# A dilated 3x3 convolution on one core: which transfers are whole, and how the last ten rows of the last image are stored

## The chip, the cores and the metric

The kernel runs on one core of one Trainium2 chip. The metric is the device time of one execution in microseconds (us); lower is better. Six runs of the kernel before stand beside a profile of one of its executions.

## The reference

Sixteen images of 64 channels and 64 x 64 pixels are convolved with 128 filters of 3 x 3 taps, dilation 2, zero padding 2, all in float32:

```python
batch, c_in, h, w, c_out, k, dilation = 16, 64, 64, 64, 128, 3, 2
x_pad = np.pad(x, ((0, 0), (0, 0), (pad, pad), (pad, pad)), mode='constant')   # pad = 2
output[b, co] += weight[co, ci, kh, kw] * x_pad[b, ci, kh*2:kh*2+h, kw*2:kw*2+w]
```

The input is 16.8 MB (1 MB an image), the output 33.6 MB (2 MB an image), the weights 0.3 MB. Every byte crosses between memory and the core once.

## The kernel before

**Pairs.** Two images of 64 channels fill the 128 partitions, so there are eight pairs, numbered 0 to 7 in the code. A pair's input is one tile `x32` of 128 partitions by 64 rows of 64 floats (2 MB). Its output is one tile `o_tiles[pb]` with the 128 output channels on the partitions and the two images side by side (4 MB).

**Groups.** A pair is worked off in four groups `g` of 16 image rows; the loop `for G in range(ngroups)` runs over 32 groups. In each, TensorE (PE) fills three PSUM tiles: `psP` (products that even and odd row blocks share), `psA` and `psB` (line 174). ScalarE (ACT) copies `psP` to `p_sb` (line 226). VectorE (DVE) adds `p_sb` to `psA` and `psB` and writes the output tile `osb` (line 233). ACT also casts the input from float32 to float16 (line 73), and DVE adds row blocks for the shared product (line 85). The order on each engine is written out by hand.

**Loads.** `load(pb, cuts, queue)` issues one transfer per piece between two cuts (line 64). The weights and pairs 0 (in two pieces), 1 and 2 are issued at the start by SyncE (SP). Pairs 3 to 7 are issued by ACT inside `casts`, as soon as the last cast of the pair three earlier has freed its `x32` tile. Pair 3 is loaded whole, pairs 4 to 7 in two halves of 32 rows.

**Stores.** `store(pb, m, r0, r1)` issues one transfer for rows `r0` to `r1` of image `m` of the pair, always over all 128 partitions, on the SP queue (line 187). Pairs 1 to 6 store two whole images after their last group. Pairs 0 and 7 store in halves: 32 rows of both images after the second group, and 32 rows of both after the fourth. In this kernel that makes 14 loads and 20 stores, 34 transfers.

**Who waits for whom.** SP issues the stores in program order, each after the DVE addition that completes its rows. There are three output tiles, so the first addition of a pair waits until the stores of the pair three earlier have landed. At the end SP waits for all stores to land (line 279 in the profile).

Of the kernel before, what the change touches and what calls it, by code (L numbers as in the profile page):

```python
# [10 lines left out]
def kernel(  # L11
# [7 lines left out]
    nc = tc.nc  # L19

    B, CI, H, W = x.shape
# [7 lines left out]
    P = 128  # L29
# [5 lines left out]
    HW = H * W  # L35
    GR = 16
    NG = H // GR
    NBLK = GR // 4
    NH = GR // 2 * W
    npairs = B // 2  # L40
    ngroups = npairs * NG
    chunk_rows = [(g * GR + (d if g else 0), min((g + 1) * GR + d, H)) for g in range(NG)]
    XF = 3
# [11 lines left out]
    out_img = out.rearrange("b o h w -> b o (h w)")  # L55
# [3 lines left out]
    x32_tiles, x16_tiles, xs_tiles, o_tiles = {}, {}, {}, {}  # L59

    def load(pb, cuts=(0, H), queue=nc.sync):
        x32_tiles[pb] = fpool.tile([P, HW], f32, tag="x32", name="x32")
        for lo, hi in zip(cuts[:-1], cuts[1:]):
            queue.dma_start(  # L64
                out=x32_tiles[pb][:, lo * W : hi * W], in_=x_pair[pb, :, lo * W : hi * W]
            )

    def cast(c):
        pb, g = divmod(c, NG)
        lo, hi = chunk_rows[g]  # L70
        if g == 0:
            x16_tiles[pb] = xpool.tile([P, HW], f16, tag="x16", name="x16")
        nc.scalar.copy(  # L73
            out=x16_tiles[pb][:, lo * W : hi * W], in_=x32_tiles[pb][:, lo * W : hi * W]
        )

    def rowsum(c):
        pb, g = divmod(c, NG)
        if g == 0:
            xs_tiles[pb] = sxpool.tile([P, HW // 2], f16, tag="xs", name="xs")  # L80
        v = x16_tiles[pb][:, g * GR * W : (g + 1) * GR * W].rearrange(
            "p (b e q) -> p b e q", e=2, q=2 * W
        )
        s = xs_tiles[pb][:, g * NH : (g + 1) * NH].rearrange("p (b q) -> p b q", q=2 * W)
        nc.vector.tensor_tensor(out=s, in0=v[:, :, 0], in1=v[:, :, 1], op=add)  # L85
# [33 lines left out]
    def turn(k):  # L119
# [24 lines left out]
        out=x16_tiles[0][:, 8 * W : 18 * W], in_=x32_tiles[0][:, 8 * W : 18 * W]  # L144
# [8 lines left out]
    def casts(G):  # L153
        for n in range(2 if G else 3):
            c = ahead[0]
            if c >= ngroups or c > G + (7 if c < 2 * NG else 3):
                return
            cast(c)
            ahead[0] += 1
            if c % NG == NG - 1 and c // NG + XF < npairs:  # L160
                k = c // NG + XF
                load(k, (0, H) if k == XF else (0, H // 2, H), queue=nc.scalar)

    def product(ps, src, kind, blk0, nblk, first, last):
        for j in (1, 0, 2):
            dw = (j - 1) * d
            o0, o1 = max(0, -dw), W - max(0, dw)
            t = kind * KW + j
            for hb in range(2):
                pp = slice(hb * CI, (hb + 1) * CI)  # L170
                rhs = src(pp, dw + o0, dw + o1)
                po = ps[:, hb * NH + blk0 * 2 * W : hb * NH + (blk0 + nblk) * 2 * W]
                po = po.rearrange("p (r w) -> p r w", w=W)[:, :, o0:o1]
                nc.tensor.matmul(  # L174
                    out=po,
                    lhsT=w_sb[pp, t * CO : (t + 1) * CO],
                    rhs=rhs,
                    start=first and j == 1,
                    stop=last and j == 2,
                )  # L180

    def blocks(x16, b0, n, e):
        v = x16.rearrange("p (b e r w) -> p b e r w", e=2, r=2, w=W)
        return lambda pp, c0, c1: v[pp, b0 : b0 + n, e, :, c0:c1]

    def store(pb, m, r0=0, r1=H):
        nc.sync.dma_start(
            out=out_img[2 * pb + m, :, r0 * W : r1 * W],
            in_=o_tiles[pb][:, m * HW + r0 * W : m * HW + r1 * W],
        )  # L190

    for G in range(ngroups):
        pb, g = divmod(G, NG)
        x16 = x16_tiles[pb]
        xs = xs_tiles[pb].rearrange("p (r w) -> p r w", w=W)
        if g == 0:
            o_tiles[pb] = opool.tile([P, 2 * HW], f32, tag="osb", name="osb")
        o = o_tiles[pb].rearrange("p (m b e q) -> p m b e q", m=2, e=2, q=2 * W)
        b0 = g * NBLK

        def summed():
            ps = ppool.tile([P, 2 * NH], f32, tag="p", name="psP")
            sv = lambda pp, c0, c1: xs[pp, g * GR // 2 : (g + 1) * GR // 2, c0:c1]
            product(ps, sv, 0, 0, NBLK, True, True)
            return ps

        if G:
            psP = summed()

        psA = apool.tile([P, 2 * NH], f32, tag="ab", name="psA")  # L210
        product(psA, blocks(x16, b0, NBLK, 1), 1, 0, NBLK, True, False)
        z = 1 if g == 0 else 0
        product(psA, blocks(x16, b0 + z - 1, NBLK - z, 1), 2, z, NBLK - z, False, True)

        psB = apool.tile([P, 2 * NH], f32, tag="ab", name="psB")
        product(psB, blocks(x16, b0, NBLK, 0), 3, 0, NBLK, True, False)
        z = 1 if g == NG - 1 else 0
        product(psB, blocks(x16, b0 + 1, NBLK - z, 0), 4, 0, NBLK - z, False, True)

        if not G:  # L220
            psP = summed()

        if not G:
            casts(0)
        p_sb = spool.tile([P, 2 * NH], f32, tag="psb", name="p_sb")
        nc.scalar.copy(out=p_sb, in_=psP)  # L226
        if G:
            casts(G)
        if G + 1 < ngroups:
            rowsum(G + 1)  # L230
        pv = p_sb.rearrange("p (m b q) -> p m b q", m=2, q=2 * W)
        for e, ps in ((0, psA), (1, psB)):
            nc.vector.tensor_tensor(  # L233
                out=o[:, :, b0 : b0 + NBLK, e],
                in0=ps.rearrange("p (m b q) -> p m b q", m=2, q=2 * W),
                in1=pv,
                op=add,
            )

        if pb in (0, npairs - 1):  # L240
            if g % 2 == 1:
                store(pb, 0, (g - 1) * GR, (g + 1) * GR)
                store(pb, 1, (g - 1) * GR, (g + 1) * GR)
        elif g == NG - 1:
            store(pb, 0)
            store(pb, 1)
# [37 lines left out]
```

## Time and profile before

| | |
|---|---|
| median of 6 runs | 127.77 us (127.59 to 127.89) |
| the profiled execution | 127.89 us, span 126.0 us, so 1.89 us lie outside the span |
| PE, DVE, ACT busy | 105.1, 90.4, 65.0 us |
| bytes moved | 50.78 MB, mean 403 GB/s over the span, in 4906 packets |
| SP's transfers | 3600 packets, 40.14 MB |
| ACT's transfers (pairs 3 to 7) | 1296 packets, 10.49 MB |
| stores | 12 of 2048 KB, 18.7 us from issue to landing; 8 of 1024 KB, 15.1 us |

The span runs from the first to the last instruction of the profiled execution. A transfer over 128 partitions moves one packet per partition: 16 KB for a whole image or pair, 8 KB for a half. The profile's rows of 40 slices show at a glance when the 16 DMA engines of the core were busy and what they moved. Each transfer also ends with a 4-byte packet on every engine that took part, which counts its completion.

### The profile page before, as it was taken

The numbers are of one execution on the slowest core, as the hardware profiler recorded it, in microseconds if no ns is written. First come the engines' busy times: TensorE is split into PE (matmuls) and PEld (weight loads), VectorE is DVE, ScalarE is ACT, GpSimd is POOL, SyncE is SP. The second block draws the span as 40 slices with busy tenths as digits, with TensorE's granted clock in tenths as the row PEclk, the third lists the DMA queues.
The fourth block names the chain that finished last, engine by engine and source line by source line (L and its number), as shares of the span: only waits on it lengthen the run. The fifth ranks groups of instructions, "written<-read, shape, count | busy, mean of one in ns | idle before, by whom it ended". The sixth has DMA issues, their size and how long they took to land.

```text
span 126.0 us, 2341 instructions
## 1 busy us (share of the span) xinstructions
PE 105.1 (83%) x1000; PEld 56.3 (45%) x1000; DVE 90.4 (72%) x103; ACT 65.0 (52%) x68; POOL 2.2 (2%) x8
## 2 busy tenths in 40 slices
PE   6994999999999999999999999999999999400000
PEld 2251555555555555555555555555555555100000
DVE  0560997988898888988969898887988987700000
ACT  4287894366656665666576666666666633000000
POOL 2400000000000000000000000000000000000000
PEclk9999999999999999999999999999999999965555
DMA  4999999999999999999999999999999999999970
GB/s 132 383 462 442 416 411 385 335 424 421 416 437 439 432 426 432 424 424 429 406 447 419 421 432 426 432 432 429 416 442 421 437 426 421 421 416 429 429 317 26
DMA packets 4906, 50.78 MB, mean 403 GB/s; under 512 B 544, under 2 KB 544, under 8 KB 800
## 3 DMA queue, kind: packets, MB, share of 16 engines
q1 hardware_dynamic: 3600, 40.14, 75.6%
q10 hardware_dynamic: 1296, 10.49, 20.4%
q8 instruction: 8, 0.13, 0.4%
q14 instruction: 2, 0.02, 0.0%
HBM read 17.07 MB, written 33.55 MB: 402 GB/s over the span
## 4 chain that ended last, share of the span: by engine, by line
PE 75%; DMA 6%; ACT 2%; issue 1%; DVE 1%; DVEq 1%; SPq 1%; ACTq 0%
PE psA L174 30%; PE psB L174 29%; PE psP L174 16%; DMA x<-in_x_dram 6%; DVE osb L233 1%; DVEq L279 1%; ACT p_sb L226 1%; ACT x L73 1%; SPq L64 0%; ACTq L64 0%; SPq L88 0%; DVEq L233 0%
## 5 line engine op out<-in xcount | busy, mean ns | idle before, releaser
L174 PEld LDWEIGHTS <-w_sb 64*128 64x128 f16 x960 | 54.2, 94 | 47.0 <-issue 2.1
L226 ACT COPY p_sb<-psP 128x1024 f32<-128x1024 f32 x32 | 32.4, 1012 | 37.5 <-PE psP L174 17.1
L233 DVE TENSOR_TENSOR osb<-psA,p_sb 128x1024 f32<-128x1024 f32 x32 | 39.2, 1224 | 14.6 <-PE psA L174 7.1
L174 PE MATMUL psA<-x,w_sb 64*128 64x496 f16 (+3 forms) x384 | 45.1, 365 | 0.1
L174 PE MATMUL psB<-x,w_sb 64*128 64x496 f16 (+3 forms) x384 | 45.1, 365 | 0.0
L233 DVE TENSOR_TENSOR osb<-psB,p_sb 128x1024 f32<-128x1024 f32 x32 | 39.0, 1220 | 0.0
L73 ACT CAST x<-x 128x1024 f16<-128x1024 f32 (+2 forms) x31 | 32.1, 1044 | 0.4 <-DMA x<-in_x_dram 0.4
L174 PE MATMUL psP<-xs,w_sb 64*128 64x496 f16 (+1 forms) x192 | 26.0, 371 | 1.8 <-ACT p_sb L226 1.8
L85 DVE TENSOR_TENSOR xs<-x 128x512 f16<-128x512 f16 x32 | 13.3, 416 | 0.7 <-ACT x L73 0.7
L101 PE MATMUL dm<-zero 128*128 128x512 f16 x10 | 4.5, 580 | 1.2 <-DVE zero L93 1.2
L111 DVE CAST wd<-w 128x192 f16<-128x192 f32 x1 | 0.5, 501 | 2.5 <-DMA w<-in_weight_dram 2.5
L101 PEld LDWEIGHTS <-zero 128*128 128x128 f16 x10 | 1.1, 123 | 2.6 <-issue 1.3
L124 PEld LDWEIGHTS <-wd 128*64 128x64 f16 x30 | 1.0, 118 | 2.2 <-DVE wd L111 1.1
L124 PE MATMUL wt<-ident,wd 128*64 128x128 f16 x30 | 1.6, 241 | 0.2 <-DVE wd L111 0.2
L113 ACT ACT_TABLE_LOAD x1 | 1.3, 1283 | 0.7 <-PEq L265 0.7
L136 ACT CAST w_sb<-wt 128x384 f16<-128x384 f32 x1 | 0.5, 479 | 1.8 <-PE wt L124 1.8
L113 ACT CAST wd<-w 128x192 f16<-128x192 f32 x1 | 0.5, 537 | 1.6 <-DMA w<-in_weight_dram 1.6
L138 DVE CAST w_sb<-wt 128x384 f16<-128x384 f32 x1 | 0.6, 557 | 0.9 <-PE wt L124 0.9
L93 DVE MEMSET zero<- 128x256 uint32 x1 | 0.3, 272 | 0.9 <-PEq L265 0.9
L112 POOL TENSOR_TENSOR wd<-w 128x192 f16<-128x192 f32 x1 | 0.8, 797 | 2.3 <-DMA w<-in_weight_dram 2.3
L115 POOL CAST wd<-w 128x192 f16<-128x192 f32 x1 | 0.8, 813 | 0.0
L114 DVE TENSOR_TENSOR wd<-w 128x192 f16<-128x192 f32 x1 | 0.8, 795 | 0.0
(11 smaller groups left out, 3.6 us busy)
## 6 DMA issues: line engine op xcount, KB each, us to landing
out_dram<-osb SPq DMA_DIRECT2D x12, 2048.0 KB, 18.7
out_dram<-osb SPq DMA_DIRECT2D x8, 1024.0 KB, 15.1
x<-in_x_dram ACTq DMA_DIRECT2D x8, 1024.0 KB, 17.5
x<-in_x_dram SPq DMA_DIRECT2D x2, 2048.0 KB, 17.7
x<-in_x_dram ACTq DMA_DIRECT2D x1, 2048.0 KB, 16.2
x<-in_x_dram SPq DMA_DIRECT2D x1, 1088.0 KB, 5.5
x<-in_x_dram SPq DMA_DIRECT2D x1, 960.0 KB, 7.3
w<-in_weight_dram SPq DMA_DIRECT2D x1, 288.0 KB, 2.8
```

The source lines that it names most:

```text
L73: nc.scalar.copy(out=x16_tiles[pb][:, lo * W : hi * W], in_=x32_tiles[pb][:, lo * W : hi * W])
L85: nc.vector.tensor_tensor(out=s, in0=v[:, :, 0], in1=v[:, :, 1], op=add)
L101: nc.tensor.matmul(out=dm[:, 0:512], lhsT=zero[:, 0:P], rhs=zero)
L112: nc.gpsimd.tensor_tensor(out=wdv[:, 3], in0=wv[:, 0], in1=wv[:, 1], op=sub)
L113: nc.scalar.copy(out=wdv[:, 2], in_=wv[:, 0])
L114: nc.vector.tensor_tensor(out=wdv[:, 1], in0=wv[:, 2], in1=wv[:, 1], op=sub)
L115: nc.gpsimd.tensor_copy(out=wdv[:, 4], in_=wv[:, 2])
L124: nc.tensor.matmul(out=wts[k % 3][r * CI : (r + 1) * CI, c0 + j * CO : c0 + (j + 1) * CO], lhsT=wd[:, t * CI : (t + 1) * CI], rhs=ident,)
L174: nc.tensor.matmul(out=po, lhsT=w_sb[pp, t * CO : (t + 1) * CO], rhs=rhs, start=first and j == 1, stop=last and j == 2,)
L226: nc.scalar.copy(out=p_sb, in_=psP)
L233: nc.vector.tensor_tensor(out=o[:, :, b0 : b0 + NBLK, e], in0=ps.rearrange("p (m b q) -> p m b q", m=2, q=2 * W), in1=pv, op=add,)
L279: with _tile.TileContext(nc) as tc:
```

## The change

1. In `casts`, pairs 4 and 5 are loaded whole, as pair 3 is; pairs 6 and 7 stay in halves.
2. Pair 0 stores two whole images after its fourth group, as pairs 1 to 6 do, and nothing after its second.
3. Of the last image (pair 7, `m` = 1), the lower half is stored in three transfers instead of one: rows 32 to 53 over all 128 partitions (5632 bytes a partition), then rows 54 to 63 (2560 bytes a partition) over partitions 0 to 123, then the same rows over partitions 124 to 127.

That makes 12 loads and 20 stores, 32 transfers. The bytes are the same.

```diff
@@ casts
-                load(k, (0, H) if k == XF else (0, H // 2, H), queue=nc.scalar)
+                load(k, (0, H) if k < 6 else (0, H // 2, H), queue=nc.scalar)

-    def store(pb, m, r0=0, r1=H):
-        nc.sync.dma_start(
-            out=out_img[2 * pb + m, :, r0 * W : r1 * W],
-            in_=o_tiles[pb][:, m * HW + r0 * W : m * HW + r1 * W],
-        )
+    def store(pb, m, r0=0, r1=H, rows=((0, P),)):
+        for lo, hi in rows:
+            nc.sync.dma_start(
+                out=out_img[2 * pb + m, lo:hi, r0 * W : r1 * W],
+                in_=o_tiles[pb][lo:hi, m * HW + r0 * W : m * HW + r1 * W],
+            )
+
+    FOUR = ((0, P - 4), (P - 4, P))
+    ROWS4 = 10

-        if pb in (0, npairs - 1):
+        if pb == npairs - 1:
             if g % 2 == 1:
                 store(pb, 0, (g - 1) * GR, (g + 1) * GR)
-                store(pb, 1, (g - 1) * GR, (g + 1) * GR)
+                if g == NG - 1:
+                    store(pb, 1, (g - 1) * GR, H - ROWS4)
+                    store(pb, 1, H - ROWS4, H, FOUR)
+                else:
+                    store(pb, 1, (g - 1) * GR, (g + 1) * GR)
         elif g == NG - 1:
             store(pb, 0)
             store(pb, 1)
```

## The prediction

> **What bounds the kernel now.** I read the slices of the page first.
>
> ```profile
> PE   6994999999999999999999999999999999400000
> PEclk9999999999999999999999999999999999965555
> DMA  4999999999999999999999999999999999999970
> GB/s 132 383 462 442 416 411 385 335 424 421 416 437 439 432 426 432 424 424 429 406 447 419 421 432 426 432 432 429 416 442 421 437 426 421 421 416 429 429 317 26
> ```
>
> PE stops at slice 34; the DMA row stays at 9 from slice 2 until slice 38. In its full slices it moves about 430 GB/s, whatever the engines do. SP's own waits say the same: its last act is 13.5 us of waiting for stores, while its waits for DVE end long before.
>
> ```profile
> SPq L279 <- DMA out_dram<-osb: 13.5, 1, 13.5
> SPq L187 <- DVE osb L233: 4.7, 1, 4.7
> ```
>
> The last store is issued at 110.2 us, when over 11 us of stores are still queued, so the compute engines are not on the path: what counts is when the last of 16 DMA engines runs dry. The windows of the tail show that they don't run dry together. The last two columns are the busy share of the 16 engines and GB/s; a packet counts in the window in which it starts.
>
> ```profile
> 121.00:121.50 0.50, 0.00 (x0) 0.00 (x0) 0.00 (x0) 0.00 (x0) 0.00 (x0) 0.50 0.74 311
> 122.00:122.50 0.50, 0.00 (x0) 0.00 (x0) 0.00 (x0) 0.00 (x0) 0.00 (x0) 0.50 0.62 262
> 122.50:123.00 0.50, 0.00 (x0) 0.00 (x0) 0.00 (x0) 0.00 (x0) 0.00 (x0) 0.50 0.20 82
> 123.00:123.50 0.50, 0.00 (x0) 0.00 (x0) 0.00 (x0) 0.00 (x0) 0.00 (x0) 0.50 0.12 49
> 124.00:124.50 0.50, 0.00 (x0) 0.00 (x0) 0.00 (x0) 0.00 (x0) 0.00 (x0) 0.50 0.12 49
> 124.50:125.00 0.50, 0.00 (x0) 0.00 (x0) 0.00 (x0) 0.00 (x0) 0.00 (x0) 0.50 0.00 0
> ```
>
> A share of 0.12 is two engines of 16. I followed the packets back from the end: on one engine each packet starts as the one before ends, and every engine has eight packets and a completion packet per transfer, so 16 chains come out. Seven engines end at 121.24 to 121.96 us, seven at 122.60 to 122.93, two at 124.46 and 124.68. The span ends 1.33 us after the last packet. All have the same bytes; what sets them apart is this row:
>
> ```profile
> q8 instruction: 8, 0.13, 0.4%
> ```
>
> Eight 16 KB packets at 16.0, 28.8, 44.3, 55.5, 69.6, 82.4, 95.7 and 108.4 us take 919 ns each on eight different engines, with another 0.3 to 0.5 us of disturbance: the seven of the middle group and the last engine. The last one also lost more than the others in a slow stretch at 20 to 24 us (315 GB/s over these 4 us, reads of 16 KB taking up to 1.4 us instead of 0.61). The second laggard took no such packet; from 37 to 110 us its packets are 3 to 8% longer, which adds up to 2.8 us.
>
> **The change part by part.** Packet periods on one chain give the prices: 607 ns for 16 KB, 306 ns for 8 KB, 6 ns for a completion packet. So a packet costs 5 ns plus 36.7 ns a KB: 212 ns for 5632 bytes, 99 ns for 2560.
>
> *Whole transfers.* Pair 0's stores: per engine 32 packets of 8 KB become 16 of 16 KB, 16 x 5 = 0.08 us, and two completions fewer, 0.01. Loads of pairs 4 and 5: the same, 0.09. Together 0.18 us less on every engine. Their timing costs nothing as long as the queues don't empty. Pair 0's first two stores move from 17.3 us to about 23.6. Until then the engines have loads: 0.3 MB of weights and five pairs of 2.1 MB last, at 430 GB/s from 2 us on, until about 27 us, and 28 with the slow stretch. The next work is issued at 35.65 us with the same bytes behind it as before; pair 0 then still had stores until 38.4 us (the median landing), so 2.8 us of cover remain. If that cover were gone, each us without work would add a us to the end. In the slow stretch the traffic from 22 to 24 us will be all reads instead of two thirds reads: A read there took 0.2 to 0.35 us longer than elsewhere and one more fits in, so I bound this at 0.4 us lost to 1.1 won (the stretch gone: 4 us x 115/430) and take zero, since the reads were slow before the first store packet ran.
>
> *Reads against stores.* Engines serve the two queues packet by packet, so a whole load with 16 KB packets gets one half beside stores instead of one third. Pair 5's load lands earlier, stores later. Who waits: pair 6's first addition already waited 0.7 us for pair 3's stores (86 us). Pair 3's second store can land no later than the last load did before (86.2 us against 85.7 on the last engine), so up to 0.5 us more for DVE there. PE stops at 108.5 and SP's last issue is at 110.2 us with 11 us of cover, so this is worth nothing at the end. For x, ACT's only load waits are at the start (0.4 us); pair 5 would be needed at about 63 us and lands before 55.
>
> *Issues.* ACT issues two transfers fewer. SP issues two fewer for pair 0 and two more at the end; one costs 0.33 to 1.56 us of SP, so the last leaves by about 114 us. The instruction records show eight completion semaphores being reused: the 31st and 32nd transfer wait at most for pair 5's stores, which landed by 100 us. Nothing but the final wait is behind them, and the engines need them only at 120.5 us.
>
> *The last ten rows.* On every engine eight packets shrink from 306 to 212 ns: 8 x 94 = 0.75 us less. The rows come back as 31 + 1 packets per engine on four engines: 32 x 99 + 12 = 3.18 us, net +2.43. No row of before has a transfer over fewer than 128 partitions; this rests on the Trainium skill, DMA: Bandwidth & Descriptors, "Why a DMA increments its semaphore by 16 and not by 1": a transfer runs on the largest number up to 16 that divides its outer dimension, and on the lowest-numbered engines; 124 and 4 both give four. By it 12 engines gain 0.75 + 0.18 = 0.93 us and four lose 2.43 - 0.18 = 2.25. If the transfers ran on 16 engines, the sum would be -0.18; on one, its 124 packets would take 12.3 us and end some 8 us later.
>
> *A rule against it.* The same page, "Rules for kernel authors", asks for 128 partitions and 1 MB a transfer, and finds small ones to be mostly overhead (about 2 us fixed each). Two more small transfers would then cost up to 4 us and turn the sum to about 131. The trace speaks otherwise: within one queue the step from one transfer to the next costs 6 ns, because the next packets are already there. I use 6 ns; the fixed part stays once, in the 1.33 us at the end.
>
> **The sum.** The laggards end at 124.68 - 0.93 = 123.75 and 123.53. Four engines of the early group would end at 121.24 to 121.96 plus 2.25, that is 123.5 to 124.2, all but one of the seven by 123.8. End about 123.8, 0.87 earlier: 127.89 - 0.87 = 127.0 for this profiled execution, which is 0.12 above the median of the runs; so 126.9 as a median.
>
> **Which four.** The records don't number the engines; all hangs on this. The point of decision is 124.68 - 2.25 = 122.43 us: a lowest engine that ended later than that before makes the kernel slower. Seven ended earlier, nine later. What speaks for the early group: the refills go to eight engines in turn, so they look like a fixed round, half of 16. The Trainium skill (Runtime: NRT & Kernel Launch, "Instruction fetch mechanics") gives PE's instruction memory as 128 KB, refilled in 16 KB blocks, so eight blocks are there before the span. If blocks go round from the lowest engine (my inference, no row shows it), the first eight took engines 0 to 7 and the eight of the span 8 to 15. For the second laggard, the DMA page ("Latency and other measured facts") has engines 7 and 15 as usually slower, though for software-made descriptors; this trace shows slow engines, not their numbers.
>
> **The rivals.**
> - *A, likeliest (0.64):* the lowest four are of the early seven: 126.9, with 126.5 to 127.4 for the ends of the slow stretch and for the engine at 121.96.
> - *B, slower (0.15):* the refills run over the lowest engines, the four are of the middle group: 122.60 to 122.93 plus 2.25 is up to 125.18, 0.5 later: 127.9 to 128.3. Against it: only the inference above.
> - *C, slower (0.10):* one of the two laggards is among the four: 124.46 or 124.68 plus 2.25, about 2.1 later: 129.7 to 130.0.
> - *D (0.07):* the ten rows run on all engines after all, or a disturbed engine moves from execution to execution so that gains and losses cancel: only the 0.18 us stay, 127.5 to 127.8.
> - *E (0.04):* an early gap or a longer slow stretch eats the gain: about 128.
>
> **How the numbers follow.** A measurement of this kernel can tell about 0.2%, 0.26 us. A is faster, and so is a little of D: 0.66. B, C and part of E are slower: 0.26. The rest, 0.08, is within. The predicted time is A's. The range from 126.4 to 128.3 holds A, B, D and E and leaves C out, and some of A's end below.
>
> **What would show it.** Right: the last packets of 2560 bytes run on four engines only, from about 120.3 to 123.7 us, the last two laggards end near 123.75, SP's final wait shrinks by about a us, and the DMA row shows no slice below 9 between 4 and 36. Wrong: a share of 0.25 (four engines) alone at the very end, longer than 124.7 us, means B or C; a share near 1 until the end means D; a dent at 24 to 38 us means that pair 0's late stores left the engines without work.

## The result and the profile after

The changed kernel gained next to nothing: 127.92 us, the median of 35 runs (127.46 to 131.72), against 127.92 us for the kernel before in 72 runs (127.59 to 130.5). The ratio is 0.9987 (95% interval 0.9975 to 0.9998), 0.13% less; 0.7% less was forecast. Single executions of the changed kernel scatter further upward (10 of the 35 took 129.4 us or more, against 4 of the 72 before), and the ratios here leave executions out that lie over 1.5% above the quickest of their kernel.

The profiled execution of the changed kernel took 129.32 us, with a span of 127.5, so it is one of the later ones; a quicker one follows with the experiments. Its slices:

```profile
PE   6794999999999999999999999999999999000000
PEclk9999999999999999999999999999999999985555
DMA  4999999999999999999999999999999999999930
GB/s 127 383 447 442 432 416 432 437 309 432 427 422 422 442 427 422 419 432 424 424 429 427 422 427 435 409 447 422 422 432 437 427 422 432 424 411 424 406 150 15
q8 instruction: 8, 0.13, 0.4%
q14 instruction: 2, 0.02, 0.0%
```

The DMA row is still full until the tail: the later stores of pair 0 left no engine without work, and 50.78 MB moved as before. The 309 GB/s in the ninth slice are the slow stretch, which has moved; the last section comes back to it. SP's final wait for stores is 12.5 us in four pieces, where it was 13.5 us in one; a store between 60 and 80 us waited 0.7 us for a landing, long before the tail.

```profile
SPq L287 <- DMA out_dram<-osb: 12.5, 4, 6.5
SPq L188 <- DVE osb L237: 4.6, 1, 4.6
SPq L188 <- DMA out_dram<-osb: 0.7, 1, 0.7
```

The tail windows (busy share and GB/s are the last two columns) show what changed:

```profile
122.00:122.50 0.50, 0.00 (x0) 0.00 (x0) 0.00 (x0) 0.00 (x0) 0.00 (x0) 0.50 0.32 125
123.00:123.50 0.50, 0.00 (x0) 0.00 (x0) 0.00 (x0) 0.00 (x0) 0.00 (x0) 0.50 0.28 89
123.50:124.00 0.50, 0.00 (x0) 0.00 (x0) 0.00 (x0) 0.00 (x0) 0.00 (x0) 0.50 0.15 58
124.00:124.50 0.50, 0.00 (x0) 0.00 (x0) 0.00 (x0) 0.00 (x0) 0.00 (x0) 0.50 0.10 41
125.00:125.50 0.50, 0.00 (x0) 0.00 (x0) 0.00 (x0) 0.00 (x0) 0.00 (x0) 0.50 0.06 26
126.00:126.50 0.50, 0.00 (x0) 0.00 (x0) 0.00 (x0) 0.00 (x0) 0.00 (x0) 0.50 0.03 10
```

About five of the 16 engines are left at 122 us (0.32 x 16), and from 124.5 us a single one (0.06) works until 126.2. Followed packet by packet, the four engines with 2560-byte packets end at 123.28, 123.70, 124.32 and 126.24 us. Of the other twelve, eleven end by 122.17 and the last, the engine with the longer packets, at 123.96.

### The profile page after: what moved, and what is told of

It is laid out like the page before. It is cut to its first block, busy times and chain, and to the rows that moved or that the text cites. A ratio compares the mean times of both kernels' runs of the same rounds, so it can differ in the third digit from the quotient of the medians.

```text
span 127.5 us, 2335 instructions
## 1 busy us (share of the span) xinstructions
PE 104.5 (82%) x1000; PEld 56.6 (44%) x1000; DVE 90.9 (71%) x103; ACT 65.0 (51%) x68; POOL 2.2 (2%) x8
## 2 busy tenths in 40 slices
DMA packets 4466, 50.78 MB, mean 398 GB/s; under 512 B 488, under 2 KB 488, under 8 KB 1000
## 3 DMA queue, kind: packets, MB, share of 16 engines
q10 hardware_dynamic: 1008, 10.49, 20.2%
## 4 chain that ended last, share of the span: by engine, by line
PE 75%; DMA 6%; ACT 2%; issue 1%; DVE 1%; DVEq 1%; SPq 1%; ACTq 0%
PE psA L174 30%; PE psB L174 29%; PE psP L174 16%; DMA x<-in_x_dram 6%; DVE osb L237 1%; DVEq L287 1%; ACT p_sb L230 1%; ACT x L73 1%; SPq L64 0%; SPq L88 0%; ACTq L64 0%; DVEq L237 0%
## 5 line engine op out<-in xcount | busy, mean ns | idle before, releaser
L146 ACT CAST x<-x 128x512 f16<-128x512 f32 x1 | 0.6, 618 | 0.3 <-DMA x<-in_x_dram 0.3
## 6 DMA issues: line engine op xcount, KB each, us to landing
out_dram<-osb SPq DMA_DIRECT2D x14, 2048.0 KB, 17.5
```

## The experiments

Theory 1: the twelve engines gained what was forecast, but the lowest four now set the end, later than the sum had them, since at least one of them takes an instruction packet of its own. Theory 2: the two small transfers have a fixed cost. Theory 3: the whole transfers lose what the split wins. Every end below is the last data packet of an engine in the profile of that run, found as in the prediction.

**The changed kernel again.** No edit.

> The changed kernel once more, beside the kernel before on one chip. Theory 1 (exposed engines: the lowest four end last, one of them took an instruction packet, and any disturbance on these four now shows in the time): the quickest executions about 0.3 us under the quickest of before (127.5 against 127.75), but a wide scatter upward, many over 128.3; the last engine of the profile is one of the lowest four, at 124.2 or later. Theory 2 (small transfers cost extra at the end): every execution carries the cost, so the scatter is no wider than before's (127.6 to 128.1 for most) and in the profile all four engines end late alike. Theory 3 (the whole transfers eat the gain): the twelve other engines are not 0.9 us earlier than before.

Measured: 127.90 us, ratio 1.0001 (0.9984 to 1.0019), quickest execution 127.46. The profiled one, at 127.53 us, shows the clean case in its tail windows:

```profile
122.50:123.00 0.50, 0.00 (x0) 0.00 (x0) 0.00 (x0) 0.00 (x0) 0.00 (x0) 0.50 0.31 125
123.00:123.50 0.50, 0.00 (x0) 0.00 (x0) 0.00 (x0) 0.00 (x0) 0.00 (x0) 0.50 0.31 125
123.50:124.00 0.50, 0.00 (x0) 0.00 (x0) 0.00 (x0) 0.00 (x0) 0.00 (x0) 0.50 0.22 88
124.00:124.50 0.50, 0.00 (x0) 0.00 (x0) 0.00 (x0) 0.00 (x0) 0.00 (x0) 0.50 0.09 36
124.50:125.00 0.50, 0.00 (x0) 0.00 (x0) 0.00 (x0) 0.00 (x0) 0.00 (x0) 0.50 0.00 0
```

A share of 0.31 is five engines: the four and the slow one. They end at 123.78, 123.84, 124.25 and 124.52, and the slow one at 123.72. The two late ones of the four are the two that took the `q14` packets (at 63.8 and 52.6 us). So the four set the end, 0.16 us before the 124.68 of the kernel before. This execution is one of the quicker ones: the median of the 14 is 0.37 us longer.

**Only the last rows on four engines.** The condition of the halves in `casts` and of pair 0's stores is put back:

```diff
-                load(k, (0, H) if k < 6 else (0, H // 2, H), queue=nc.scalar)
+                load(k, (0, H) if k == XF else (0, H // 2, H), queue=nc.scalar)
-        if pb == npairs - 1:
+        if pb in (0, npairs - 1):
-                if g == NG - 1:
+                if pb and g == NG - 1:
```

> Only the last ten rows on four engines; pair 0 stored in halves and pairs 4 and 5 loaded in halves as before. Theory 1: quickest executions 0.1 to 0.2 us under before's, the same wide scatter upward as the changed kernel, since the scatter belongs to the split. Theory 2: no quicker than before in any execution, scatter as before. Theory 3: clearly faster than the changed kernel, about 127.0, with before's scatter.

Measured: 128.31 us, ratio 1.0012 (0.9992 to 1.0031). The four end at 123.78, 123.88, 124.46 and 125.06, again with the `q14` packets (57.8 and 52.6 us) on the two last; the slow engine ends at 123.80. It is not faster than the changed kernel, where theory 3 had expected about 127.0, so theory 3 fails here. For the two of its four without an instruction packet the packet rates give about 123.7 (121.24 + 2.43, without the 0.18 us of the whole transfers); they end within 0.2 us of it, which leaves no room for theory 2's cost.

**Only the whole transfers.**

```diff
-                if g == NG - 1:
-                    store(pb, 1, (g - 1) * GR, H - ROWS4)
-                    store(pb, 1, H - ROWS4, H, FOUR)
-                else:
-                    store(pb, 1, (g - 1) * GR, (g + 1) * GR)
+                store(pb, 1, (g - 1) * GR, (g + 1) * GR)
```

> Only the whole transfers (pair 0 stored in whole images, pairs 4 and 5 loaded whole); the last rows over 16 engines as before. The prediction's price is 0.18 us less: about 127.6 to 127.7 against 127.8 to 127.9. Theory 1: that, with before's narrow scatter. Theory 2: the same as theory 1. Theory 3: slower than before, by 0.5 us or more, or with the wide scatter of the changed kernel.

Measured: 127.89 us, ratio 0.9990 (0.9973 to 1.0007), quickest 127.45. The forecast 0.18 us (0.14%) lies in the interval, and so does zero. Theory 3's loss of 0.5 us (ratio 1.004) does not. The single profile (128.58 us) ends with the slow engine at 125.40, and its executions scattered more than theory 1 had said: 127.45 to 129.78. A wide scatter was the other sign that had been named for theory 3, so a part of the scatter may belong to the whole transfers.

**The last ten rows cut off, but over all 16 engines.**

```diff
-                    store(pb, 1, H - ROWS4, H, FOUR)
+                    store(pb, 1, H - ROWS4, H)
```

> The changed kernel with the last ten rows as a transfer of their own, but over all 128 partitions and so over all 16 engines: one transfer fewer than the changed kernel, nothing moved between engines. Theory 1: as with the whole transfers alone, 0.1 to 0.3 us under before, last packets at the engines' old order; a cut costs 8 x 5 + 6 = 0.05 us an engine. Theory 2: about 2 us later than the whole transfers alone, or half of that. Theory 3: as the whole transfers alone, whatever that is.

Measured: 127.90 us, ratio 0.9997 (0.9972 to 1.0021). Nothing is lost by the cut that could be told, and nothing won: the slow engine is alone at the end again, at 124.73, the others end at 121.06 to 123.12. Theory 2's fixed cost of a us or two per small transfer is out for a transfer over all engines.

**Twenty rows on the four.** `ROWS4 = 20`.

> The changed kernel with twenty rows instead of ten on the four engines: a check of the price of a row. By the packet price (5 ns and 36.7 ns a KB) 32 packets of 5120 bytes take 6.2 us instead of 3.2, and 0.75 us more are given up: 2.3 us later on the four engines than with ten rows. Theory 1 (the lowest four set the end): last packets at 126.1 to 126.9 us, time 129.8 to 130.1. Theory 2 (a fixed cost of the small transfers sets it): later by less than 1 us. Theory 3 (the whole transfers set it): the time does not move.

Measured: 130.15 us, ratio 1.0160 (1.0121 to 1.0200). Its tail windows:

```profile
123.50:124.00 0.50, 0.00 (x0) 0.00 (x0) 0.00 (x0) 0.00 (x0) 0.00 (x0) 0.50 0.27 113
124.50:125.00 0.50, 0.00 (x0) 0.00 (x0) 0.00 (x0) 0.00 (x0) 0.00 (x0) 0.50 0.27 113
125.50:126.00 0.50, 0.00 (x0) 0.00 (x0) 0.00 (x0) 0.00 (x0) 0.00 (x0) 0.50 0.25 102
126.00:126.50 0.50, 0.00 (x0) 0.00 (x0) 0.00 (x0) 0.00 (x0) 0.00 (x0) 0.50 0.13 51
```

Four engines in 16 (0.25) work alone until 126.13 to 126.45 us, and the slow one of the others ends at 123.32. So the rows run on four engines, at the price of the packet rates; theory 2 had expected less than 1 us more than with ten rows, and theory 3 none.

**Seven engines instead of four.**

```diff
-    FOUR = ((0, P - 4), (P - 4, P))
-    ROWS4 = 10
+    SEVEN = ((0, 119), (119, P))
+    ROWS4 = 12
```

> The last twelve rows over partitions 0 to 118 (119 = 7 x 17, so seven engines by the rule) and then 119 to 127 (nine engines). Each of the seven takes 18 packets of 3072 bytes, 2.13 us, and gives up 0.9: net +1.2; the others give up 0.9. Theory 1: if the engine with the longer packets (124.46 in the profile of before) is not among the lowest seven, the seven end at 122.3 to 123.2 and that engine at 123.4: about 126.8 to 127.2, the quickest of all. If it is among them, it ends at 125.5 and the time is 128.7 or more. Theory 2: the same number of transfers as the changed kernel, so the same time as it. Theory 3: the same time as the changed kernel.

Measured: 129.21 us, ratio 1.0094 (1.0069 to 1.0119): the second of the two cases. Its tail windows:

```profile
123.50:124.00 0.50, 0.00 (x0) 0.00 (x0) 0.00 (x0) 0.00 (x0) 0.00 (x0) 0.50 0.18 74
124.50:125.00 0.50, 0.00 (x0) 0.00 (x0) 0.00 (x0) 0.00 (x0) 0.00 (x0) 0.50 0.12 49
125.00:125.50 0.50, 0.00 (x0) 0.00 (x0) 0.00 (x0) 0.00 (x0) 0.00 (x0) 0.50 0.06 25
125.50:126.00 0.50, 0.00 (x0) 0.00 (x0) 0.00 (x0) 0.00 (x0) 0.00 (x0) 0.50 0.02 6
```

The last engine, at 125.70, has the longer packets up to 110 us and then 17 + 1 packets of 3072 bytes: the slow engine is one of the lowest seven. The slow engine had no 2560-byte packets in the ten-row kernels, so it is not one of the lowest four.

**The kernel before, profiled again.** No edit.

> The kernel before, profiled once more, to see which of its two late engines comes back. Theory 1: the engine with 3 to 8% longer packets between 37 and 110 us comes back and ends at about 124.4; the engine that took the first instruction packet at 16 us ends with the middle group or late, as it happens, so only part of the 124.68 was there to be won in every execution. Rivals: both come back alike (then a full 0.9 us was to be won), or neither (then the ends are drawn anew in each execution).

Measured: 128.01 us, ratio 0.9985 (0.9951 to 1.0020). The tail windows:

```profile
122.50:123.00 0.50, 0.00 (x0) 0.00 (x0) 0.00 (x0) 0.00 (x0) 0.00 (x0) 0.50 0.28 115
123.00:123.50 0.50, 0.00 (x0) 0.00 (x0) 0.00 (x0) 0.00 (x0) 0.00 (x0) 0.50 0.08 33
123.50:124.00 0.50, 0.00 (x0) 0.00 (x0) 0.00 (x0) 0.00 (x0) 0.00 (x0) 0.50 0.04 16
124.00:124.50 0.50, 0.00 (x0) 0.00 (x0) 0.00 (x0) 0.00 (x0) 0.00 (x0) 0.50 0.08 33
```

Only one engine is late now, the slow one at 124.68. The engine with the first instruction packet ends at 123.05 among the others. The five engines without any instruction packet and at the usual rate end at 121.32 to 121.56, the two with a `q14` packet at 121.95 and 122.42.

**Fewer rows.** `ROWS4 = 5`, then 3, 7 (twice) and 8.

> The changed kernel with five rows instead of ten on the four engines. Per engine of the four, 31 + 1 packets of 1280 bytes at 52 ns are 1.68 us, less 0.38 us given up: net +1.3 instead of +2.43; the other twelve give up 0.38 instead of 0.75. Theory 1: the four end near 122.4 to 123.1, the laggards near 124.1; quickest executions about 127.3 to 127.4, and a narrower scatter than with ten rows because the four have a us of slack again: median 0.3 to 0.5 us under before. Theory 2: the number of transfers is the same, so the same extra cost: no faster than the changed kernel. Theory 3: same as the changed kernel.

> The changed kernel with three rows on the four engines. Theory 1: the slow engine gives up 0.18 + 0.23 us and sets the end at about 124.3, the four end at 122.0 to 123.1 with a us of slack: time about 0.3 us under before, with before's narrow scatter, and between five rows and the whole transfers alone. Theory 2 (a fixed cost of the small transfers): as ten rows. Theory 3: as the whole transfers alone.

> The changed kernel with seven rows on the four engines. Theory 1, by the ends measured so far (slow engine of before 124.7, four lowest 121.3 to 122.4): the slow engine gives up 0.18 + 0.53 us and ends at about 124.0; the four take 32 packets of 1792 bytes at 71 ns, 2.28 us, less 0.53 and 0.18, so they end at 122.9 to 124.0. Both ends meet: quickest executions about 127.2, 0.1 us under five rows, but the four have no slack left and the median is at five rows' or up to 0.3 us above. Theory 2 (a fixed cost of the small transfers): as five and ten rows. Theory 3: as the whole transfers alone.

> Seven rows once more, to see whether the gain stands in another set of runs. Theory 1: 127.0 to 127.5, about 0.5% under before. Rivals (a small transfer's fixed cost, or the whole transfers, set the end): the first seven-row runs were a lucky draw, and these lie where five and three rows lay, 0.2% under before.

> Eight rows on the four engines. Theory 1: the four end 0.24 us later than with seven rows (123.2 to 124.3, the ones with an instruction packet last), the slow engine 0.08 us earlier: 0.1 to 0.3 us above seven rows, 0.2 to 0.5 under ten, with some scatter upward. Rivals: no order between seven, eight and ten.

Measured, with ten and twenty rows beside them:

| rows on the four | median us | ratio to before (95%) | last of the four | slow engine |
|---|---|---|---|---|
| 3 | 127.77 | 0.9985 (0.9971 to 0.9999) | 122.85 | 124.38 |
| 5 | 127.65 | 0.9980 (0.9969 to 0.9991) | 123.90 | 124.31 |
| 7 | 127.16 | 0.9938 (0.9915 to 0.9960) | 123.93 | 123.81 |
| 7, again | 127.63 | 0.9968 (0.9945 to 0.9991) | 124.15 | 124.47 |
| 8 | 127.82 | 0.9991 (0.9959 to 1.0023) | 123.96 | 124.08 |
| 10 | 127.92 | 0.9987 (0.9975 to 0.9998) | 126.24 | 123.96 |
| 10, again | 127.90 | 1.0001 (0.9984 to 1.0019) | 124.52 | 123.72 |
| 20 | 130.15 | 1.0160 (1.0121 to 1.0200) | 126.45 | 123.32 |

With 3 and 5 rows the slow engine is last, with 10 and 20 the four; with 7 and 8 they meet within 0.4 us. Seven rows is faster than the kernel before in two sets of runs, by 0.6 and 0.3%; only the first set is clear of the intervals with ten rows as well. The second set's median lies above the 127.0 to 127.5 that had been expected of it. Where the intervals overlap (3, 5, 7 again, 8) the order is not shown. The tail of the first seven-row profile (span 125.2 us) has no work after 124 us:

```profile
123.00:123.50 0.50, 0.00 (x0) 0.00 (x0) 0.00 (x0) 0.00 (x0) 0.00 (x0) 0.50 0.26 99
123.50:124.00 0.50, 0.00 (x0) 0.00 (x0) 0.00 (x0) 0.00 (x0) 0.00 (x0) 0.50 0.09 34
124.00:124.50 0.50, 0.00 (x0) 0.00 (x0) 0.00 (x0) 0.00 (x0) 0.00 (x0) 0.50 0.00 0
```

## Why the prediction was wrong

**What bounds the kernel: right.** The last DMA engine sets the end in each profile; from its last packet to the end of the span are 1.17 to 1.51 us in all of them.

**The price of the rows, and the rule of four engines: right.** With ten rows, the two of the four without an instruction packet end at 123.78 and 123.84 in the clean profile, and 123.5 to 123.8 came out for such engines. From ten to twenty rows a step of 2.3 us was worked out; the two that took no `q14` packet moved from 123.78 and 123.84 to 126.13 and 126.45, 2.3 to 2.6 us. That a transfer costs 6 ns on top of its packets, and not the 2 us of the rule against it, stands too: the cut over all engines lost nothing that could be told. (On the page named there, the 2 us are a fit for single transfers issued from gpsimd, and stand outside its rules.)

**The laggards: right within the scatter of a profile.** "123.75 and 123.53" were forecast, the second for the slow engine; it ended at 123.72 and 123.96 in the profiles of the changed kernel and at 123.80 with the split alone. In the second profile of before it ends at 124.68, which gives 123.75. The other late engine of before was no fixture: it did not come back when before was profiled again. As the slow engine alone ends there at 124.68, the gain to be had is the same.

**Which four: right in its main inference, wrong in a detail that decided.** In all nine profiles with rows on the four, followed back packet by packet, none of PE's `q8` packets fell on the lowest four, and none of the four is the slow engine, so these are of the early group. But both `q14` packets fell on two of the four, in all nine. In before such a packet costs its engine 0.3 us for itself and 0.1 to 0.36 us of disturbance: those engines end at 121.55 and 121.96 in the first profile, at 121.95 and 122.42 in the second.

**The step that failed is the sum's choice for the four:** "that is 123.5 to 124.2, all but one of the seven by 123.8. End about 123.8". The end is a maximum over four engines, not the likeliest of them, and the two of the early group with a `q14` packet are among them. The prediction had the 124.2 in hand for one of them and left it to the range. With the second profile's ends the same working gives 122.42 + 2.25 = 124.67 us, which is the 124.68 of before: no gain. So in that execution an engine with a `q14` packet, and so presumably one of the four, stood at the point of decision that the prediction had named, 122.43; that the hundredths agree is luck. In the clean ten-row profile the four end at 124.52, 0.7 us after the 123.8 of the sum and 0.16 us before the slow engine of before, and that execution took 127.53 us. This explains 0.6 of the 1.0 us between the 126.9 of the prediction and the median of 127.92; the other 0.4 us are scatter, and their cause is open. The 0.13% measured are 0.17 us, about what rival D gave (only the 0.18 us of the whole transfers stay), but not by D's cause: the rows did run on four engines.

**The whole transfers: their price is not contradicted** (0.18 us forecast, 0.13 with an interval of -0.09 to 0.35), and their cover held. The slow stretch was rightly costed at nothing, but not for the reason given. The reads are slow before the first store packet runs, as the prediction said; it took from this that the stretch stays where it is, and it moved by about 5 us, costing as much as before (last section).

**Two figures without weight in the sum:** the eight instruction packets take 879 to 968 ns, 930 on average, where the prediction has 919 each; and its 36.7 ns are for 1000 bytes.

**What stays open:** in the first profile of the changed kernel one of the four ended at 126.24. Four of its packets at 59 to 75 us lost 0.8 us, and four of its packets between 121.4 and 123.4 us lost 1.4 us. Where these come from was not settled. If any engine may be hit so, ten rows leave four engines without slack for it, where before there were one or two. That this widens the scatter fits three rows and the first seven-row runs (narrower), but eight rows and the second seven-row runs went up to 129.25 us, and the whole transfers alone scattered too, so it is not shown.

## What to carry to other kernels

When transfers bound a kernel, look at each DMA engine's own end: the time is the latest of 16, and bytes moved to engines that finish early gain only down to the next engine in line. Work out the end for the latest of the engines that take the work, and from more than one profile; leave them some slack: here seven rows gained 0.3 to 0.6%, and ten at most 0.25%. This kernel, at its transfer bound all through, gained a few tenths of a per cent from such a shift and no more.

## What the runs showed of the hardware

**One DMA engine is steadily slower.** In each profile one engine's 16 KB packets take about 640 ns instead of 611 until PE stops at 108 to 110 us, 3.2 to 3.5 us in all from 30 us on. By the runs over four and over seven engines it is one of the lowest seven and not of the lowest four. It keeps the usual rate once the compute engines are done; the cause was not looked for. The prediction had weighed the Trainium skill (DMA: Bandwidth & Descriptors, "Latency and other measured facts": engines 7 and 15 are usually slower), which ties this to descriptors made by software; here SP and ACT issue every transfer, on queues that the profile calls `hardware_dynamic`. With engines counted from 0, the seven-engine run puts the slow one at 4 to 6, so it is neither of the two.

**Instruction packets keep to certain engines.** PE's eight packets went to eight different engines, in all nine profiles none of the lowest four and not the slow one; the two `q14` packets fell on two of the lowest four in each.

**A slow stretch comes with the first stores.** Reads of 16 KB take up to 1.4 us for some 3 us, once, costing each engine about 0.9 us. The first read of over 750 ns starts at 20.2 us in before, at 25.0 in the changed kernel and at 20.3 in the kernel with only the split. The first store is issued at 17.3, 23.2 and 17.5 us, and the first store packet runs at 22.8, 27.0 and 22.8 us: the stretch begins after the issue, but before any store packet runs. The windows of before (share and GB/s last):

```profile
20.00:24.00 4.00, 4.00 (x44) 2.35 (x42) 3.27 (x6) 2.02 (x2) 0.00 (x0) 1.00 0.97 315
24.00:28.00 4.00, 4.00 (x42) 2.14 (x39) 3.58 (x4) 2.06 (x2) 0.00 (x0) 1.00 1.00 420
```

The same windows of the changed kernel:

```profile
20.00:24.00 4.00, 4.00 (x44) 2.30 (x42) 3.42 (x6) 1.60 (x2) 0.00 (x0) 1.00 0.99 422
24.00:28.00 4.00, 4.00 (x41) 2.17 (x38) 3.58 (x4) 2.06 (x2) 0.00 (x0) 1.00 1.00 340
```

And of the kernel with only the split:

```profile
20.00:24.00 4.00, 4.00 (x44) 2.30 (x41) 3.25 (x6) 2.02 (x2) 0.00 (x0) 1.00 1.00 334
24.00:28.00 4.00, 4.00 (x40) 2.17 (x38) 3.59 (x5) 2.06 (x2) 0.00 (x0) 1.00 1.01 422
```

The dent of the last column (315, 340, 334) moves with the first store and keeps about its depth. The kernel with only the split puts back pair 0's stores and the half loads of pairs 4 and 5 together, so these runs do not tell which of the two moves it; what makes the reads slow was not tried.
